# First RMS norm of a streaming encoder step: all squares on ScalarE, the depthwise weights' load moved behind the second half of the input, one weight tile's low parts on VectorE alone

## The chip, the cores and the metric

The kernel runs on one core of a Trainium2 chip. The metric is the device time of one execution in microseconds (us); the time before is the median of three runs. Engines are named as the profile names them: PE (TensorE matrix products; PEld is its weight load), DVE (VectorE), ACT (ScalarE), POOL (GpSimd) and SP (SyncE, which here only issues DMAs). Each engine works through its own queue in program order and waits on semaphores for the others.

## The reference

One inference step of a small encoder trunk: one layer with a convolution module and an FFN, one layer with chunked attention and an FFN, all in float32. What matters here is only its start:

```python
def rms_norm(x, g):
    xf = x.astype(jnp.float32)
    y = xf * lax.rsqrt(jnp.mean(xf * xf, axis=-1, keepdims=True) + EPS)
    return (y * g.astype(jnp.float32)).astype(x.dtype)

def conv_module(h, hist, g, w_pw1, b_pw1, w_dw, b_dw, ln_g, ln_b, w_pw2, b_pw2):
    a, gate = jnp.split(rms_norm(h, g) @ w_pw1 + b_pw1, 2, axis=-1)
    glu = a * jax.nn.sigmoid(gate)
    ...
```

The model width is 1024. There are 512 prompt frames and 8 x 16 sample frames, 640 columns in all. The depthwise convolution that follows uses the weights `w_dw` of width 31.

## The kernel before

Activations are kept with features on the 128 partitions: `h` is [128, 8, 640], so feature tile k (0 to 7) of a frame is one column. The 640 frames are worked on in two halves of 320 columns, g = 0 and g = 1.

**Products in three parts.** Every float32 operand is split into a high part (rounded to fp32r by ScalarE: `whi` for weights, L178; `xh` for activations, L190) and a low part (the difference, by VectorE: `wlo`, L183; `xl`, L192). A product is three PE matmuls, high x high, high x low and low x high (`mm3`, L202 to L204), each with 320 moving columns. `L243` are small matmuls that sum a norm's squares over the partitions, `L257` those that spread the resulting 1/rms back to all partitions, and `L149` (`warm`) are matmuls of the identity whose results nobody uses.

**First norm (`rms(0, ...)`, L298).** The input half g = 0 comes in four DMAs of two feature tiles each (`load_x`, L121, SP's queue). Each of the eight tiles is squared: by ScalarE (L211) where the letter in the string `SSQ` is `a`, by VectorE (L214) where it is `v`. VectorE adds the squares up in tile `acc` (L233). The squares' tiles `sq` rotate through two buffers, so that a square waits until the square two places before it has been added. Then: column sums on PE (L243), epsilon added on VectorE (L280, `rst`), power -0.5 on GpSimd (L287), spread on PE (L257), and for each k the scaled tile `n` on VectorE (L309), its `xh` on ScalarE and its `xl` on VectorE.

**Warm matmuls.** `WARM = 30, 9, 5, 0`: 30 identity matmuls stand in PE's queue ahead of the column sums, 9 between the sums and the spread, 5 behind the spread. Each is two records in the trace.

**Weights.** `w_pw1` comes in eight tiles of [128, 2048], `raw` (L164, SP's queue). The first two, `pws[0]` and `pws[1]`, are loaded and split in four pieces of 512 columns (`wsplit`, L152). The tuple `PL1` says how many quarters of a tile's low parts GpSimd takes in VectorE's place: for tile 1 it is 2, so of each piece VectorE makes 256 columns and GpSimd 256. The argument `ties` names earlier instructions behind which the split is to stand in its engines' queues; it sets an order, and adds no wait of its own.

**The first products.** `PLAN` (L75) starts with `a0 y x1 b0 b1`: `a0` is weight tile 0 with half 0 (48 matmuls), `y` loads input half 1 (`load_x(1)`, `in_xb`), `x1` is weight tile 1 with half 0 (48 matmuls), in whose middle the second half's norm is put (`mid`, L1056), and `b0`, `b1` are the same weight tiles with half 1. A scheduler with a time model of its own places the instructions in each engine's queue; PE takes the first half of `x1` in turn with `a0` and needs `n`, `xh` and `xl` of tile k as it goes. 72 matmuls of 320 columns stand between the spread and the second half's column sums (the second group of `L243`).

**The second half's norm (g = 1).** All eight squares are on ScalarE (`SSQ1`, L211), and GpSimd adds them up (L233, written as `w<-w,sq` in the trace since the sum is kept in a `w4` buffer). `behind(norm_end["xh"][2], ...)` puts these squares behind the third `xh` of the first half.

**The depthwise weights.** `dwv` [128, 504] is loaded by ScalarE's DMA queue (L781). In the trace it is first used by GpSimd at L890 (29.0 us).

Of the kernel before, what the change touches and what calls it, by code (L numbers as in the profile page):

```python
# [44 lines left out]
CUT, LCUT = 8, (7, 7)  # L45
GAPS, GAPS1 = (1, 12, 2), (5, 3, 12, 4)
POOLED = 14, 21, 26, W
PL1 = (0, 2, 0, 0, 0, 0, 0, 0)
PL2 = (0, 0)
M2 = ((0, 1, 2, 3), (2, 3, 0, 1))  # L50
SQ = 'aaaaaaaa'
# [1 line left out]
CVT = 4  # L53
HA = T + NB * SB - 320 - NB * SB
NXA, NXB = NB * SEG + HIST + HA, HIST + 320
SSQ = 'avavavaa'
SCUT = 8
CB, QB = 7, 1
NSTD = 3
# [10 lines left out]
SETS = "k1 v1 k2 k3 o0 k4 v2 k5 o1 k6 v3 k7 o2"  # L70
LAG = 1
SSQ1 = 'aaaaaaaa'
WARM = 30, 9, 5, 0
LNO = ((0, 1, 4, 5, 6, 3, 2, 7), (0, 1, 4, 2, 3, 5, 6, 7))
PLAN = ("a0 y x1 b0 b1 q0 dp1s0 c2 ds1p2 D3 C4 S3 q3 C5 E6 u S4 A4 F6 u k ds2 B4 E7 e S5 A5 F7 f k k k S6 A6 "  # L75
        "p S7 A7 n s0 m w1")
# [4 lines left out]
V_NKV, V_NATT, V_NFFN, V_NFIN, V_N = 56, 64, 72, 88, 96  # L81
# [4 lines left out]
def tile_trunk(ctx, tc, xT, vecs, hist, w_pw1, w_pw2, w_in0, w_out0, w_os0, w_in1, w_out1, w_os1,  # L86
               w_kq, w_v, w_o, rel, kc, vc, y_out, convp_out, convs_out, k_out, v_out):
    nc = tc.nc
# [27 lines left out]
    norm_end = {"xh": [], "n": [], "t": None}  # L116

    def load_x(g):
        g0, n = gr[g]
        for k in range(0, KT, 2):  # L120
            norm_end["x"] = nc.sync.dma_start(h[:, k:k + 2, g0:g0 + n], xT[g][:, k:k + 2, :]).ins  # L121
# [17 lines left out]
    @contextmanager  # L139
    def behind(*ins):  # L140
        with ExitStack() as st:
            for i in ins:
                st.enter_context(tc.issue_after(i))
            yield

    def warm(n):
        pt = mmt()
        for _ in range(n):
            end = nc.tensor.matmul(pt[:, 0:P], ident, ident, start=True, stop=True)  # L149
        return end.ins  # L150
# [43 lines left out]
    def new_xs(g):  # L194
        n = gr[g][1]
        return (xp.tile([P, KT, n], F32R, tag=f"xh{g}", name=nm("xh")),
                xp.tile([P, KT, n], F32R, tag=f"xl{g}", name=nm("xl")))
# [100 lines left out]
    def rms(g, gain, engs=SQ, cut=CUT, eng=nc.gpsimd, hold=None, hook=None):  # L298
# [3 lines left out]
        xh, xl = new_xs(g)  # L302
        if WARM[2 + g]:
            with behind(norm_spread[0]):
                warm(WARM[2 + g])
        for k in range(KT):
# [442 lines left out]
    dwv = cp.tile([P, V_NDW], F32, name="dwv", tag="dwv")  # L749

    def load_hist(c0, c1):
        nc.sync.dma_start(gs[:, c0:c1], hist[:, c0:c1])
# [17 lines left out]
    def first():  # L770
        with behind(mean_end[0]):
            warm(WARM[1])
        pws[0] = wsplit(w_pw1[0], 16, P, cuts=4, pool=PL1[0],
                        ties=[(norm_end["sq"], norm_end[e]) for e in ("acc", "acc", "rst", "rst")])

    with tc.issue_after(warm(WARM[0])), tc.high_priority(offset=2 * HP):
        xs = [rms(0, V_NCONV, SSQ, SCUT, nc.vector, hook=first), None]
    pws[1] = wsplit(w_pw1[1], 16, P, cuts=4, pool=PL1[1],
                    ties=(norm_end["sq"], norm_end["n"][3], norm_end["pow"]))
    load_hist(0, 2)  # L780
    nc.scalar.dma_start(dwv, vecs[:, V_N:])  # L781

    def w4t():
        return cp.tile([P, 1024], F32, tag="w4", name=nm("w4"), bufs=3)
# [256 lines left out]
    def step(op, arg):  # L1041
# [5 lines left out]
        elif op == "c":  # L1047
            w = pws.get(c) or wsplit(w_pw1[c], 16, P, pool=PL1[c], cuts=2)
            pws[c + 1] = wsplit(w_pw1[c + 1], 16, P)
# [2 lines left out]
            glu(c, 1, *w)  # L1052
        elif op == "y":
            load_x(1)
        elif op == "x":
            def mid(some):  # L1056
                def hook():
                    with tc.issue_after(mean_end[0]):
                        cover[:] = [some()]

                with behind(norm_end["xh"][2], norm_end["pow"]):
                    xs[1] = rms(1, V_NCONV, SSQ1, 8, hold=w4t, hook=hook)
            glu(1, 0, *pws[1], mid=mid)
        elif op in "CDEF":
            if op != "F":
# [73 lines left out]
    for tok in PLAN.split():  # L1139
        step(tok[0], tok[1:])  # L1140
# [459 lines left out]
    for p in range(NP):  # L1600
# [8 lines left out]
        for op in BO[p].split():  # L1609
# [11 lines left out]
            i = int(op[1]) if len(op) > 1 else None  # L1621
# [29 lines left out]
    with tc.high_priority(offset=HP):  # L1651
        sqs = xp.tile([P, KT, 384], F32, tag="xl1", name=nm("sqs")).rearrange("p a n -> p (a n)")
        acc, r = sqs[:, KT * NH:(KT + 1) * NH], sqs[:, (KT + 1) * NH:(KT + 1) * NH + 8]
        for k in range(KT):
            sq = square(h[:, k, 0:NH], NH, "a", sqs[:, k * NH:(k + 1) * NH])
# [103 lines left out]
    acc, bsb, bcs, sq, rs = {}, {}, {}, {}, {}  # L1759
# [117 lines left out]
```

## Time and profile before

| what | us |
|---|---|
| time before, median of three runs (1431.62 to 1432.91) | 1431.68 |
| the profiled execution's own time | 1431.78 |
| its span in the profile | 1430.0 |
| PE busy, share of the span | 1416.8, 99% |
| VectorE busy | 1113.5, 78% |
| ScalarE busy | 746.9, 52% |
| GpSimd busy | 278.4, 19% |

PE counts as busy in the warm matmuls too, and the ends of matmuls are modelled, so short waits hide in the 99%. The span is what the hardware profiler saw of the engines; 1.78 us of the profiled execution's time lie around it. A timeline row gives start, duration, engine, line, operation, output and inputs, shape and count; a row that merges several instructions gives their common stretch. In a bracket at a row's end stands how long the engine sat idle and what ended that.

### The profile page before, as it was taken

How to read it: one execution, taken by the hardware profiler on the slowest of the kernel's cores; microseconds unless marked ns; L12 is line 12 of the kernel's file. 1: busy time of each engine (PE TensorE's matmuls, PEld its weight loads, DVE VectorE, ACT ScalarE, POOL GpSimd, SP SyncE). 2: the span in 40 equal slices, each digit the busy share in tenths (PEclk: the TensorE clock that was granted, in tenths of full speed). 3: DMA queues.
4: the chain of work that ended last, by engine and by line, in shares of the span. 5: the costliest groups of instructions: out<-in, count | busy, mean ns of one | idle time of the engine just before them, and what ended most of it. 6: DMA issues, size and time to landing. Idle time of an engine off the chain costs nothing.

```text
span 1430.0 us, 28700 instructions
## 1 busy us (share of the span) xinstructions
PE 1416.8 (99%) x11076; PEld 1364.0 (95%) x11076; DVE 1113.5 (78%) x2490; ACT 746.9 (52%) x1633; POOL 278.4 (19%) x335
## 2 busy tenths in 40 slices
PE   9999999999999999999999999999999999999998
PEld 9998799999999999999998998888999999999998
DVE  7799867898888888765666757667898798798765
ACT  5666554554653554545654554544564564464453
POOL 5699121011111110112111111110011111111101
PEclk9999999999999999999999999999999999999999
DMA  7267424154644644524456555561244544554522
GB/s 248 91 176 187 123 84 143 32 122 122 169 107 121 148 115 117 139 89 174 165 185 205 187 179 173 181 218 51 60 108 118 147 125 110 145 131 109 135 72 74
DMA packets 93722, 192.62 MB, mean 135 GB/s; under 512 B 15121, under 2 KB 45585, under 8 KB 90129
## 3 DMA queue, kind: packets, MB, share of 16 engines
q1 hardware_dynamic: 79216, 160.59, 36.0%
q0 software_dynamic: 13504, 29.37, 10.5%
q8 instruction: 87, 1.43, 0.4%
q10 hardware_dynamic: 864, 0.83, 0.2%
q14 instruction: 51, 0.41, 0.1%
HBM read 179.14 MB, written 11.61 MB: 133 GB/s over the span
## 4 chain that ended last, share of the span: by engine, by line
PE 93%; DVE 4%; ACT 1%; issue 1%; DMA 1%; POOL 0%; DVEq 0%; ACTq 0%; POOLq 0%
PE mm L451 52%; PE mm L1311 11%; PE mm L202 6%; PE mm L204 6%; PE mm L203 6%; PE mm L923 3%; PE w L1311 2%; PE am L1484 1%; PE am L1556 1%; PE am L1500 1%; PE w L1455 1%; PE w L1518 1%; PE w L243 1%; PE mm L149 1%; PE w L257 1%
## 5 line engine op out<-in xcount | busy, mean ns | idle before, releaser
L451 PE MATMUL mm<-XH,whi 128*128 128x320 f32 x896 | 275.9, 310 | 1.0 <-ACT t L463 0.7
L451 PE MATMUL mm<-XH,wlo 128*128 128x320 f32 x896 | 276.2, 309 | 0.0
L451 PE MATMUL mm<-XL,whi 128*128 128x320 f32 x896 | 274.7, 309 | 0.0
L375 ACT ACTIVATE whi<-raw 128x512 fp32r<-128x512 f32 (+2 forms) x280 | 167.5, 613 | 148.4 <-PE mm L451 91.9
L376 DVE TENSOR_TENSOR wlo<-raw,whi 128x512 fp32r<-128x512 f32 (+2 forms) x280 | 183.8, 667 | 29.8 <-ACT whi L375 29.2
L451 PE MATMUL mm<-hid,whi 128*128 128x320 f32 x732 | 170.9, 310 | 0.0
L451 PEld LDWEIGHTS mm<-XH,whi 128*128 128x128 f32 x896 | 167.7, 188 | 2.8 <-ACT t L463 1.5
L451 PEld LDWEIGHTS mm<-XH,wlo 128*128 128x128 f32 x896 | 168.2, 188 | 0.0
L451 PEld LDWEIGHTS mm<-XL,whi 128*128 128x128 f32 x896 | 167.7, 188 | 0.0
L202 PE MATMUL mm<-xh,whi 128*128 128x320 f32 (+2 forms) x416 | 128.8, 312 | 0.5 <-DVE h L733 0.4
L203 PE MATMUL mm<-xh,wlo 128*128 128x320 f32 (+2 forms) x416 | 128.0, 309 | 0.0
L204 PE MATMUL mm<-xl,whi 128*128 128x320 f32 (+2 forms) x416 | 125.5, 310 | 1.0 <-DVE xl L192 1.0
L451 PEld LDWEIGHTS mm<-hid,whi 128*128 128x128 f32 x732 | 124.8, 188 | 1.5 <-DVE h L602 0.9
L451 PE MATMUL mm<-hid,wlo 128*128 128x320 f32 x366 | 113.0, 309 | 0.0
L451 PE MATMUL mm<-XH,shi 128*128 128x320 f32 x344 | 106.2, 310 | 1.2 <-DVE h L1588 0.7
L451 PE MATMUL mm<-XH,slo 128*128 128x320 f32 x344 | 106.0, 308 | 0.0
L602 DVE TENSOR_TENSOR h<-h,mm 128x320 f32<-128x320 f32 x168 | 79.1, 482 | 34.2 <-PE mm L451 34.2
L451 PE MATMUL mm<-XL,shi 128*128 128x320 f32 x344 | 105.6, 308 | 0.0
L375 ACT ACTIVATE shi<-raw 128x512 fp32r<-128x512 f32 (+1 forms) x114 | 66.4, 588 | 59.6 <-PE mm L451 31.6
L879 POOL TENSOR_TENSOR ca<-ca,cvt 128x512 f32<-128x512 f32 x60 | 89.5, 1492 | 17.3 <-ACT cvt L876 11.1
L428 POOL DMA_DIRECT2D s<-in_w_in x38 | 22.0, 578 | 309.1 <-ACT shi L375 67.3
L376 DVE TENSOR_TENSOR slo<-raw,shi 128x512 fp32r<-128x512 f32 (+1 forms) x114 | 72.0, 636 | 12.4 <-ACT shi L375 12.0
(337 smaller groups left out, 3663.1 us busy)
## 6 DMA issues: line engine op xcount, KB each, us to landing
raw<-in_w_in SPq DMA_DIRECT2D x152, 256.0 KB
s<-in_w_in POOLq DMA_DIRECT2D x76, 256.0 KB, 4.3
raw<-in_w_os SPq DMA_DIRECT2D x96, 192.0 KB
cache<-in_ck SPq DMA_DIRECT2D x32, 512.0 KB
cache<-in_cv SPq DMA_DIRECT2D x32, 512.0 KB
raw<-in_w_pw SPq DMA_DIRECT2D x11, 1024.0 KB
s<-in_w_os POOLq DMA_DIRECT2D x48, 192.0 KB, 3.6
raw<-in_w_kq SPq DMA_DIRECT2D x8, 1024.0 KB
```

What stands on the lines that cost most here:

```text
L149: end = nc.tensor.matmul(pt[:, 0:P], ident, ident, start=True, stop=True)
L202: nc.tensor.matmul(ps, wh, xh, start=(first and i == 0), stop=False)
L203: nc.tensor.matmul(ps, wl, xh, start=False, stop=False)
L204: end = nc.tensor.matmul(ps, wh, xl, start=False, stop=(stop and i == last))
L375: put_end[1] = nc.scalar.activation(out=hi, in_=src, func=AF.Copy).ins
L376: put_end[0] = nc.vector.tensor_tensor(out=lo, in0=src, in1=hi.bitcast(F32), op=sub).ins
L428: nc.gpsimd.dma_start(s1, src[:, 2 * n:3 * n])
L451: last = nc.tensor.matmul(pt, wt, v, start=(first and k == i == 0), stop=(k == n - 1 and i == 2), skip_group_check=True)
L602: hadd[i, u] = [nc.vector.tensor_tensor(out=hv, in0=hv, in1=pt, op=sub if row else add).ins]
L879: nc.gpsimd.tensor_tensor(out=acc, in0=acc, in1=pr, op=ALU.add)
L923: conv_end[0] = nc.tensor.matmul(pt[32 * q:32 * q + 32, 0:n], w4[0:r, 4 * tg + q, :], mv, start=(tg == 0), stop=(tg == 7)).ins
L1311: step_end[0] = nc.tensor.matmul(ps, w, x, start=i == j == 0, stop=i == len(wts) - 1 and j == 2).ins
```

## The change

Five places are edited.

- `SSQ` goes from `avavavaa` to `aaaaaaaa`: VectorE's three squares of the first norm go to ScalarE.
- `WARM[0]` goes from 30 to 21.
- `PL1[1]` goes from 2 to 0: GpSimd makes no low parts of weight tile 1 any more, VectorE makes all four pieces with 512 columns each.
- The ties of weight tile 1's split change: piece i (0 to 3) is placed behind `xh` of tile i + 1, where before all four pieces were placed behind the last square of the first norm.
- `dwv` is loaded on SP's queue behind the four DMAs of input half 1 (`y`), where it was on ScalarE's DMA queue at the program's start; and the second half's squares are placed behind the second `xh`, where they were behind the third.

```diff
-PL1 = (0, 2, 0, 0, 0, 0, 0, 0)
+PL1 = (0, 0, 0, 0, 0, 0, 0, 0)
-SSQ = 'avavavaa'
+SSQ = 'aaaaaaaa'
-WARM = 30, 9, 5, 0
+WARM = 21, 9, 5, 0
...
     pws[1] = wsplit(w_pw1[1], 16, P, cuts=4, pool=PL1[1],
-                    ties=(norm_end["sq"], norm_end["n"][3], norm_end["pow"]))
+                    ties=[(norm_end["xh"][i], norm_end["n"][3], norm_end["pow"])
+                          for i in range(1, 5)])
     load_hist(0, 2)
-    nc.scalar.dma_start(dwv, vecs[:, V_N:])
...
         elif op == "y":
             load_x(1)
+            nc.sync.dma_start(dwv, vecs[:, V_N:])
...
-                with behind(norm_end["xh"][2], norm_end["pow"]):
+                with behind(norm_end["xh"][1], norm_end["pow"]):
                     xs[1] = rms(1, V_NCONV, SSQ1, 8, hold=w4t, hook=hook)
```

What this makes of the queues shows best on VectorE, in the stretch where the first half's tiles are scaled and split (`n` scaled, `xl` low part, `wlo_239` or `wlo_230` the low part of weight tile 1). Before:

```order
L309 SCALAR_TENSOR_TENSOR n_23_213<-h,vec,w_2_137 128x320
L309 SCALAR_TENSOR_TENSOR n_24_217<-h,vec,w_2_137 128x320
L183 TENSOR_TENSOR wlo_239<-raw_237,whi_238 128x256 x4
L192 TENSOR_TENSOR xl_198<-n_23_213,xh_197 128x320
L192 TENSOR_TENSOR xl_198<-n_24_217,xh_197 128x320
L309 SCALAR_TENSOR_TENSOR n_25_221<-h,vec,w_2_137 128x320
```

VectorE, the same place of the changed program:

```order
L309 SCALAR_TENSOR_TENSOR n_23_204<-h,vec,w_2_128 128x320
L309 SCALAR_TENSOR_TENSOR n_24_208<-h,vec,w_2_128 128x320
L183 TENSOR_TENSOR wlo_230<-raw_228,whi_229 128x512
L192 TENSOR_TENSOR xl_189<-n_23_204,xh_188 128x320
L183 TENSOR_TENSOR wlo_230<-raw_228,whi_229 128x512
L192 TENSOR_TENSOR xl_189<-n_24_208,xh_188 128x320
L309 SCALAR_TENSOR_TENSOR n_25_212<-h,vec,w_2_128 128x320
L183 TENSOR_TENSOR wlo_230<-raw_228,whi_229 128x512
L309 SCALAR_TENSOR_TENSOR n_26_216<-h,vec,w_2_128 128x320
L192 TENSOR_TENSOR xl_189<-n_25_212,xh_188 128x320
L183 TENSOR_TENSOR wlo_230<-raw_228,whi_229 128x512
```

Four pieces of 256 columns in a row have become four pieces of 512 columns, spread among the low parts of tiles 2 to 4. On ScalarE, from the first weight tile's high parts (`whi_180`) on, before (`sq_347` and later are squares of the second half):

```order
L178 ACTIVATE whi_180<-raw_179 128x512 x4
L178 ACTIVATE whi_238<-raw_237 128x512 x4
L190 ACTIVATE xh_197<-n_21_205 128x320
L190 ACTIVATE xh_197<-n_22_209 128x320
L190 ACTIVATE xh_197<-n_23_213 128x320
L211 ACTIVATE sq_347<-h 128x320
L211 ACTIVATE sq_349<-h 128x320
```

ScalarE in the changed program (`whi_171` is weight tile 0, `whi_229` weight tile 1, `sq_334` the second half's first square):

```order
L178 ACTIVATE whi_171<-raw_170 128x512 x4
L190 ACTIVATE xh_188<-n_21_196 128x320
L190 ACTIVATE xh_188<-n_22_200 128x320
L178 ACTIVATE whi_229<-raw_228 128x512
L211 ACTIVATE sq_334<-h 128x320
L211 ACTIVATE sq_336<-h 128x320
L190 ACTIVATE xh_188<-n_23_204 128x320
L178 ACTIVATE whi_229<-raw_228 128x512
L190 ACTIVATE xh_188<-n_24_208 128x320
L178 ACTIVATE whi_229<-raw_228 128x512
```

The high parts of weight tile 1 have moved from ahead of the first `xh` to places between the `xh`, and the second half's first two squares stand ahead of the third `xh`. On GpSimd the four `L183` rows are gone and nothing else moves. On SP `dwv` stands behind the fourth `in_xb` load. On PE the same 72 products stand between spread and sums, with a few low-part products in other places. From there to the start of the first FFN every engine's order is the same; there, over some 500 of PE's 9219 rows, some rows change places with their neighbours, because the scheduler's time model had moved, and behind them the order is the same again.

## The prediction

> **What bounds the kernel now.** I read the span and the chain that ended last first, then who PE waited for (in all, how often, the longest).
>
> ```profile
> span 1430.0 us, 28700 instructions
> PE 93%; DVE 4%; ACT 1%; issue 1%; DMA 1%; POOL 0%; DVEq 0%; ACTq 0%; POOLq 0%
> PE mm L204 <- DVE xl L192: 1.0, 2, 0.5
> PE mm L451 <- DVE h L1588: 0.7, 1, 0.7
> ```
>
> The chain is PE's. Once its real products run, PE hardly stops: behind low parts `xl` twice, 0.5 each, and nowhere for more than 0.7. So the whole edit is worth what it does to one clock reading: the time at which PE has the first 72 products behind it and reaches the second half's column sums. What comes after keeps its length. The next view is the timeline of PE and its weight loads.
>
> ```profile
> 1.63 8.76 PEld L149 LDWEIGHTS mm<-ident 128*128 128x128 f32 x60 [1.63 <-POOL ident masks.py:199]
> 10.31 0.75 PEld L243 LDWEIGHTS w<-onec,acc 128*128 128x128 f32 x6
> 10.98 2.09 PEld L149 LDWEIGHTS mm<-ident 128*128 128x128 f32 x18
> 12.99 0.75 PEld L257 LDWEIGHTS w<-ident,rst 128*128 128x128 f32 x6
> 15.07 0.19 PEld L202 LDWEIGHTS mm<-xh,whi 128*128 128x128 f32 x1 [0.21 <-ACT xh L190]
> 27.13 0.72 PE L243 MATMUL w<-onec,w 128*128 128x1 f32 x6
> 38.46 0.31 PE L202 MATMUL mm<-xh,whi 128*128 128x320 f32 x1
> 43.89 0.31 PE L202 MATMUL mm<-xh,whi 128*128 128x320 f32 x1
> ```
>
> Real work starts at 15.07 and the second sums at **27.13**. The 60 warm records end where the first sums begin (10.31), and the 18 next ones where the spread begins (12.99): in both places PE's own queue, not only the data, sets the time. A product costs 0.147 (37 of them from 38.46 to 43.89), so 72 cost 10.6; 12.06 passed, and 1.5 were waits.
>
> **Part 1, the first norm sooner.** Behind the sums stand VectorE's additions; here is its timeline with ScalarE's squares and the load that is moved.
>
> ```profile
> 4.28 0.47 ACT L211 ACTIVATE sq<-h 128x320 f32<-128x320 f32 x1 [1.30 <-DMA h<-in_xa]
> 4.88 0.49 DVE L233 TENSOR_TENSOR acc<-sq,sq 128x320 f32<-128x320 f32 x1
> 5.98 0.49 DVE L214 TENSOR_TENSOR sq<-h 128x320 f32<-128x320 f32 x1 [0.61 <-DMA h<-in_xa]
> 6.48 0.49 DVE L233 TENSOR_TENSOR acc<-acc,sq 128x320 f32<-128x320 f32 x1
> 9.06 0.49 DVE L233 TENSOR_TENSOR acc<-acc,sq 128x320 f32<-128x320 f32 x1
> 9.65 0.49 DVE L233 TENSOR_TENSOR acc<-acc,sq 128x320 f32<-128x320 f32 x1
> 11.27 0.15 DVE L280 TENSOR_SCALAR rst<-w 128x3 f32<-128x3 f32 x1
> 11.50 1.25 POOL L287 TENSOR_TENSOR rst<-rst,mhalf 128x3 f32<-128x3 f32 x1 [8.93 <-DVE rst L280]
> 13.97 0.55 DVE L309 SCALAR_TENSOR_TENSOR n<-h,vec,w 128x320 f32<-128x320 f32 x1 [1.35 <-PE w L257]
> dwv<-in_vecs ACTq DMA_DIRECT2D x1, 252.0 KB
> 3.00:4.00 1.00, 1.00 (x7) 1.00 (x6) 0.00 (x0) 0.00 (x0) 0.00 (x0) 1.00 1.05 397
> ```
>
> The input's first pair of tiles is used at 4.28, the second at 5.98. From 3 us on the DMA engines are full at 397 GB/s, so `dwv` takes 258 KB / 397 = 0.65 us from the input. Without it the second pair comes between 5.33 (all of `dwv` was ahead) and 5.98 (none), the first between 3.63 and 4.28; I take 5.35 and 4.0, since both loads are issued in the same two microseconds.
>
> Now all squares are on ScalarE. Two of them and their sum take 4.0 + 0.41 + 0.47 + 0.05 + 0.49 = 5.4; the third square may then have its buffer and starts at 5.45, and the second addition at 5.95 (6.48 before). Five more follow. Additions that wait for ScalarE and for VectorE's own last result go 0.59 apart (9.06 to 9.65), and ScalarE with 0.47 a square keeps up. The last ends at 5.95 + 5 x 0.59 + 0.49 = **9.4 to 9.5**, before 10.14; the bounds are 9.05 and 9.9. Taking three squares (0.49 each) from VectorE thus brings less than their sum, for the slower pace takes part of it back.
>
> The 18 records fewer at 0.111 take 2.0 off the warm stretch: it ends near 8.35 and no longer sets anything, PE idles about 1.1 us. From the last addition to epsilon it is 11.27 - 10.14 = 1.13 (two low parts of weight tile 0 stand between), then 0.23 and 1.25 for the power: 9.45 + 2.61 = 12.06. On PE it is 0.67 for the sums and 2.01 for the nine warm ones: 9.5 + 2.68 = 12.18, a little later, as before. So spread, first `n` and first product come **0.8 sooner** (bounds 0.3 and 1.1): 12.18, 13.17, 14.27. The high parts of weight tile 1 that ScalarE no longer makes ahead of the first `xh` give nothing, since that `xh` waited for `n`.
>
> **Part 2, the products behind it.** VectorE must feed them, and it gets more to do. Its rows, ScalarE's and GpSimd's:
>
> ```profile
> 15.01 0.47 ACT L190 ACTIVATE xh<-n 128x320 fp32r<-128x320 f32 x1
> 17.14 0.82 ACT L211 ACTIVATE sq<-h 128x320 f32<-128x320 f32 x2
> 9.36 2.17 ACT L178 ACTIVATE whi<-raw 128x512 fp32r<-128x512 f32 x4
> 11.34 1.28 DVE L183 TENSOR_TENSOR wlo<-raw,whi 128x512 fp32r<-128x512 f32 x2
> 15.05 0.81 DVE L192 TENSOR_TENSOR xl<-n,xh 128x320 fp32r<-128x320 f32 x1
> 17.10 0.41 DVE L183 TENSOR_TENSOR wlo<-raw,whi 128x256 fp32r<-128x256 f32 x1
> 18.03 0.89 POOL L233 TENSOR_TENSOR w<-sq,sq 128x320 f32<-128x320 f32 x1 [2.52 <-ACT sq L211]
> 18.11 1.10 DVE L183 TENSOR_TENSOR wlo<-raw,whi 128x256 fp32r<-128x256 f32 x1
> 19.13 0.48 DVE L192 TENSOR_TENSOR xl<-n,xh 128x320 fp32r<-128x320 f32 x1
> 19.53 1.20 DVE L192 TENSOR_TENSOR xl<-n,xh 128x320 fp32r<-128x320 f32 x1
> 20.65 0.54 DVE L309 SCALAR_TENSOR_TENSOR n<-h,vec,w 128x320 f32<-128x320 f32 x1
> 21.11 0.54 DVE L309 SCALAR_TENSOR_TENSOR n<-h,vec,w 128x320 f32<-128x320 f32 x1
> 24.77 1.16 DVE L192 TENSOR_TENSOR xl<-n,xh 128x320 fp32r<-128x320 f32 x1
> 25.66 1.00 POOL L233 TENSOR_TENSOR w<-w,sq 128x320 f32<-128x320 f32 x1
> 29.00 1.91 POOL L890 TENSOR_TENSOR w<-i,dwv 128x1024 f32<-128x1024 f32 x1
> ```
>
> A low part takes 0.41 or 0.48 alone, and 1.1 to 1.2 when it starts just after one of GpSimd's sums (18.11 behind 18.03): it is held 0.70 until the sum is done; four were, the first at 18.11, the last at 24.77. `n`, which reads PSUM, is not held. From start to start VectorE pays 0.46 for an `n` (20.65 to 21.11), 0.40 for an `xl` (19.13 to 19.53), 0.34 for 256 columns of `wlo` (three from 17.10 to 18.11) and, two taking 1.28, 0.60 for 512. Before: 8 x 0.46 + 8 x 0.40 + 4 x 0.34 = 8.2 of the 11.96 from 13.97 to the last `xl`'s end, 24.77 + 1.16 = 25.93. The other 3.7 are four holds of 0.70, one of 0.33 behind GpSimd's low part (15.05), and 0.6 for `xh` and the like. Now the four `wlo` cost 2.4 in place of 1.36, in all **9.3**. GpSimd's low parts and the hold of 0.33 go; but the longer pieces stand where GpSimd's seven sums now run, from about 16 us on (the second `xh` still ends 1.5 behind the first `n`, at 14.7; then a high part of 2.17 / 4 = 0.54 and two squares, 0.82). I keep 3.7 (about half a hold more); the bounds are 2.8, four holds alone, and 4.9, all seven sums with one hold each. The last `xl` ends at 13.17 + 9.3 + 3.7 = 26.2 (25.3 to 27.4), **a quarter microsecond later than before although VectorE starts 0.8 sooner**.
>
> PE has three products behind the last `xl`: 0.06 to start (15.01, where one `xh` ends and the next begins, to the product's load at 15.07) + 3 x 0.147 = 0.5, so the second sums cannot start before 26.7 (25.8 to 27.9). Before, this floor was 26.4, and 27.13 came out, because PE had been stopped earlier (one of the two waits of 0.5, among others). With stops of that kind the new time lies between 26.7 and 27.3; I take 27.0, **0.1 sooner than 27.13**. Which end it is hangs on a race: whether VectorE's first 512-column piece or GpSimd's first sum starts first, both near 16.05.
>
> Of the rest: GpSimd's sums must be done by then; the last one ended at 26.66, 0.5 ahead of PE, and with the first one 2 us sooner (18.03 to 16.05) they end ahead of the last `xl`, hidden. `dwv` now follows the second half's input, which the row at 25.66 shows to have been there before; 0.65 more is still ahead of 29.0, where GpSimd first reads it. PE's other wait of 0.5 comes in the second half's products, whose queues keep their order, and stays. The new order of rows at the first FFN moves products among neighbours whose inputs PE did not wait for; I cost it at nothing, and bound it by the longest wait that PE has there or anywhere behind the start, 0.7, to the bad side and 0.2 to the good one.
>
> The Trainium skill, "SBUF — State Buffer", section "Who interferes with whom", says that a VectorE instruction with two SBUF inputs and a GpSimd instruction that reads SBUF exclude each other, the later one blocking until the first is done. By that rule all twelve two-input parts are exposed, not only those that met a sum before; with seven sums it gives the upper bound above. The held rows agree with it (1.10 in place of 0.41).
>
> **The rivals.**
>
> 1. *The start's gain stays* (chance 0.2). The race goes VectorE's way throughout, with four holds or fewer, and PE reaches the sums at 25.9 to 26.5: 1430.4 to 1431.0. For it speaks that PE's floor leaves room; against it that VectorE has 1.0 more to do.
> 2. *VectorE becomes the bound, slower* (0.15). Six or seven sums hold a low part; each hold beyond the fifth puts 0.70 on the last `xl`. From the sixth on it decides: PE at 27.4 to 27.9, 1432.0 to 1432.5.
> 3. *PE's clock drops in the new idle microsecond* (0.04). At the start the same warm records come at half the pace:
>
> ```profile
> 5.00:6.00 1.00, 1.00 (x7) 1.00 (x7) 0.39 (x2) 0.02 (x1) 0.00 (x0) 1.00 1.05 371
> 6.00:7.00 1.00, 1.00 (x12) 1.00 (x11) 0.97 (x2) 0.45 (x1) 0.00 (x0) 1.00 0.99 339
> ```
>
> 7 records in a microsecond and, from 6 us, 12. If the 1.1 us without work brought that back, the 24 records to the spread would cost 24 x 0.1 = 2.4 more, the start would come 1.6 later than before, and up to 2 us more would go in the products: 1433 to 1435. The trace has two stops of 0.5 and products 0.147 apart behind the second; nothing as long as 1.1 is in it. The Trainium skill, "TensorE: Matmul & The Clock Gate", section "What's actually happening", puts the fall at an idle window of about 3.4 us; by that rule 1.1 us costs nothing.
> 4. *The first norm does not move* (0.06): `dwv` took nothing from the input, and additions at 0.59 end at 9.9. The start gains 0.3, VectorE's 9.3 + 3.7 stay, and the second sums come at 27.3 to 27.8: 1431.9 to 1432.3.
>
> **How the numbers follow.** The profiled execution took 1431.78 (the span and 1.78 around it), 0.1 above the median of the three runs, 1431.68. PE's reading of 27.0 takes 0.1 from either: I forecast **1431.6** on the median, with a chance of 0.55 and 1431.0 to 1432.0 of its own. The range takes rival 1 with the lower FFN bound and the lowest run, and rivals 2 and 4 with the upper FFN bound and the spread of the runs: 1430.0 to 1433.2. A measurement of this kernel tells about 0.2%, 2.9 us, from no change. The gain on hand is at most 1.1 at the start and 1.5 of waits, so *faster* needs all of both and more: 0.02. *Slower* needs rival 3 at its worst or an unseen stop: 0.04. *Same*: 0.94.
>
> **What would show it.** In the changed kernel's profile: the last first-half addition ending at 9.4 to 9.5, the first product near 14.3, low parts of 1.1 us and more beside GpSimd's sums, the last first-half `xl` ending near 26.2, and second sums near 27.0. Additions 0.5 apart, or a second pair at 4.9, would make part 1 too small; sums at 26 would show VectorE's waits overrated; warm records 0.21 apart behind 9 us would be rival 3; a new PE stop between 200 and 400 us, the FFN's order.

## The result, and the profile after

The changed kernel takes 1435.81 us (median of 11 runs, 1433.31 to 1436.63); the kernel before, beside it on the same chip, 1431.59 (1430.95 to 1432.91). The ratio is **1.0025, 95% interval 1.0015 to 1.0034**: slower by some 3.6 us, clear of the noise, though with a quarter of a per cent still inside what the forecast called *same*. I had forecast 1431.6 with a range up to 1433.2. The profiled execution is the shortest of the 11: 1433.31, with a span of 1431.4. It therefore shows only part of the loss, and a second one was needed (below).

The page of the changed kernel, span and chain, and then whom PE waited for:

```profile
span 1431.4 us, 28664 instructions
PE 91%; DVE 4%; DMA 2%; ACT 1%; issue 1%; POOL 0%; SPq 0%; DVEq 0%; ACTq 0%
```

```profile
PE mm L204 <- DVE xl L192: 1.2, 2, 0.8
PE w L243 <- DVE acc L233: 0.7, 1, 0.7
```

36 instructions fewer are the nine matmuls taken out (each two weight loads and two matmuls). The chain's DMA share went from 1% to 2%, which asks for a transfer that had not been waited for. The waits for low parts are about what they were (1.2, before 1.0), and the one ahead of the sums is the idle time of the start. First the start, on PE and VectorE:

```profile
1.62 7.18 PE L149 MATMUL mm<-ident 128*128 128x128 f32 x42 [1.62 <-POOL gall L761]
9.48 0.83 PE L243 MATMUL w<-onec,acc 128*128 128x1 f32 x6 [0.67 <-DVE acc L233]
12.37 0.93 PE L257 MATMUL w<-ident,rst 128*128 128x128 f32 x6
14.45 0.41 PE L202 MATMUL mm<-xh,whi 128*128 128x320 f32 x1
26.98 0.72 PE L243 MATMUL w<-onec,w 128*128 128x1 f32 x6
7.14 2.28 DVE L233 TENSOR_TENSOR acc<-acc,sq 128x320 f32<-128x320 f32 x4 [0.20 <-ACT sq L211]
21.31 1.36 DVE L183 TENSOR_TENSOR wlo<-raw,whi 128x512 fp32r<-128x512 f32 x1
24.24 1.67 DVE L192 TENSOR_TENSOR xl<-n,xh 128x320 fp32r<-128x320 f32 x2
```

The additions end at 7.14 + 2.28 = 9.42, the first product starts at 14.45, the last low part ends at 25.91, the second sums start at 26.98. The start came out close to the forecast, and up to 470 us PE stays 0.1 to 0.3 ahead of the kernel before. The time goes at two places of the first FFN. PE there, and the chain into the second place:

```profile
477.56 0.31 PE L451 MATMUL mm<-XL,whi 128*128 128x320 f32 x1
478.34 0.42 PE L451 MATMUL mm<-XH,whi 128*128 128x320 f32 x1 [0.47 <-ACT whi L375]
478.95 0.42 PE L451 MATMUL mm<-XH,shi 128*128 128x320 f32 x1 [0.19 <-DVE h L602]
589.92 0.31 PE L451 MATMUL mm<-XL,whi 128*128 128x320 f32 x1
590.69 0.41 PE L451 MATMUL mm<-XH,shi 128*128 128x320 f32 x1 [0.46 <-ACT shi L375]
591.29 0.41 PE L451 MATMUL mm<-XH,whi 128*128 128x320 f32 x1 [0.19 <-DVE h L602]
```

```profile
584.82 4.59 DMA raw<-in_w_in
589.49 0.64 ACT whi L375
```

Products that should follow 0.15 apart start 0.78 and 0.61 apart (0.77 and 0.60 at the second place): 0.94 and 1.0 lost against the kernel before. PE waits for a high part that ScalarE makes (L375) of a weight block loaded by SP (L424), 4.59 from issue to landing. ScalarE's rows show how much later that load is; the first pair is the kernel before, the second the changed one:

```profile
476.53 0.63 ACT L375 ACTIVATE shi<-raw 128x512 fp32r<-128x512 f32 x1 [2.69 <-DMA raw<-in_w_in]
587.87 0.63 ACT L375 ACTIVATE whi<-raw 128x512 fp32r<-128x512 f32 x1 [2.60 <-DMA raw<-in_w_in]
```

```profile
477.14 0.63 ACT L375 ACTIVATE shi<-raw 128x512 fp32r<-128x512 f32 x1 [3.62 <-DMA raw<-in_w_in]
589.49 0.63 ACT L375 ACTIVATE whi<-raw 128x512 fp32r<-128x512 f32 x1 [3.61 <-DMA raw<-in_w_in]
```

ScalarE idles 3.6 instead of 2.6. At the first place the trace has fifteen of the load's sixteen parts landed by 475.71 and the last at 477.07. At the second place the fifteenth lands 3.52 behind the issue and the last 4.59. What is new beside the load is a packet of the kind *instruction*, on queue q8, taken here to be PE's own program (the runs below test that). The DMA view between 586.8 and 587.8 of the changed kernel (packets, then queue and kind: packets, MB, share of 16 engines):

```profile
DMA packets 166, 0.32 MB, mean 324 GB/s; under 512 B 16, under 2 KB 16, under 8 KB 165
q8 instruction: 1, 0.02, 5.5%
```

One packet of 16 KB, 5.5% of 16 engines for 1.0 us, or 0.88 us of one engine. It starts at 586.85, 2.0 behind the load's issue. Before, the packet started at 583.17, 1.0 ahead of the issue (584.20).

### The profile page after: what moved, and what is told of

Read it like the earlier page. It is cut to its first block, busy times and chain, and to the rows that moved or that the text cites. A ratio compares the mean times of both kernels' runs of the same rounds, so it can differ in the third digit from the quotient of the medians.

```text
span 1431.4 us, 28664 instructions
## 1 busy us (share of the span) xinstructions
PE 1416.0 (99%) x11058; PEld 1362.3 (95%) x11058; DVE 1113.0 (78%) x2487; ACT 747.2 (52%) x1636; POOL 275.4 (19%) x331
## 4 chain that ended last, share of the span: by engine, by line
PE 91%; DVE 4%; DMA 2%; ACT 1%; issue 1%; POOL 0%; SPq 0%; DVEq 0%; ACTq 0%
PE mm L451 51%; PE mm L1312 11%; PE mm L202 6%; PE mm L204 6%; PE mm L203 6%; PE mm L923 3%; PE w L1312 2%; PE am L1485 1%; PE am L1557 1%; PE am L1501 1%; PE w L1456 1%; PE w L1519 1%; DMA raw<-in_w_in 1%; PE w L243 1%; DVE wlo L376 1%
## 5 line engine op out<-in xcount | busy, mean ns | idle before, releaser
L375 ACT ACTIVATE whi<-raw 128x512 fp32r<-128x512 f32 (+2 forms) x280 | 167.8, 613 | 150.3 <-PE mm L451 92.8
L375 ACT ACTIVATE shi<-raw 128x512 fp32r<-128x512 f32 (+1 forms) x114 | 66.3, 588 | 62.8 <-PE mm L451 33.4
```

Source lines behind the costliest of these rows:

```text
L375: put_end[1] = nc.scalar.activation(out=hi, in_=src, func=AF.Copy).ins
```

## The experiments

The theories, by the letters of the expectations. **A**: PE's program is fetched in such packets; with fewer instructions ahead of a point, the packet fetched there comes later against the work, and now meets a weight load that PE needs soon. **B**: the idle time at the start lowers PE's clock. **C**: the rest of the change costs the time. **D**, from the third set on: PE's clock falls to half for one stretch of 3.41 us when PE does little for about half of such a stretch, at the start and elsewhere. Every kernel was timed in 11 runs except two (8 and 5). The edits are against the change, unless another base is named.

**The change once more, and three kernels on its warm matmuls.** The first has the change unedited.

> The changed kernel once more. Theory A (PE's instruction fetch): two groups of PE stops, near 478 and 590 us, 0.6 to 0.8 each, behind a weight load whose last part lands 1.3 late on one DMA engine while a 16 KB instruction packet passes; they alone make 1433.3. Theory B (PE's clock falls in the new idle microsecond at 8.5 to 9.5): most executions are 1434.6 to 1436.6 and show PE products 0.29 apart in place of 0.147 for some 3.4 us, near the start. Rival C (the start itself): second sums later than 27.2 in the slow executions, without either.

Measured: 1434.87 (1433.25 to 1436.52), ratio 1.0020 [1.0011, 1.0029]. The profile is of its longest execution, 1436.52, and shows what the first one lacked. Stretches of 1 us: PE, PEld, DVE, ACT, POOL, then the granted clock, the DMA share and GB/s:

```profile
590.00:591.00 1.00, 0.68 (x5) 0.42 (x3) 0.00 (x0) 0.02 (x1) 0.00 (x0) 1.00 0.73 133
593.00:594.00 1.00, 1.00 (x4) 1.00 (x5) 1.00 (x3) 0.63 (x2) 0.00 (x0) 0.50 0.00 0
594.00:595.00 1.00, 1.00 (x5) 1.00 (x5) 1.00 (x2) 0.52 (x1) 0.00 (x0) 0.50 0.12 8
596.00:597.00 1.00, 1.00 (x8) 1.00 (x7) 1.00 (x3) 0.33 (x2) 0.31 (x1) 0.88 0.17 61
```

The packet here took 2.05 us, the high part started 5.7 behind the load's issue, and PE stopped for 1.81 and 0.60. Then the clock was 0.5 from 592.82 to 596.24, and four or five products went into a microsecond instead of seven. This place alone cost 3.5; another 0.4 went at 478, and 0.5 at 316.

```diff
-WARM = 21, 9, 5, 0
+WARM = 30, 9, 5, 0      # warm30
+WARM = 21, 18, 5, 0     # count
```

> The changed kernel with 30 warm matmuls in place of 21; all else as in the change, and the order at the first FFN is then that of before. PE has as many instructions ahead of every later place as before, and no idle microsecond ahead of the first sums. A: no stops at 478 and 590. B: no slow executions, all within 1.5. First sums near 10.3, first product near 15.1, second sums 27.3 to 27.8, so 1431.7 to 1432.3. Rival C: as slow as the change, 1435 to 1436.

Measured: 1432.39 (1431.92 to 1437.14), ratio 1.0011 [1.0002, 1.0020]; no stop at 478 or 590, though the first sums come at 10.96. The second sums come at 28.60, later than the 27.3 to 27.8 expected. Two of the 11 runs take 1436.20 and 1437.14, at a mean clock of 0.998; neither was profiled, so what lengthens them is open.

> The changed kernel with 21 warm matmuls ahead of the first sums and 18 in place of 9 behind them: the idle microsecond stays, PE has the 30 instructions of before in all, and the other engines have the order of the 30-warm kernel. The nine cost 2.0 at the start: second sums 28.4 to 29.2, 1432.9 to 1433.6 by that alone. A: no stops at 478 and 590. B: the slow executions stay, median 2 to 3 above that, 1435 to 1436.5.

Measured: 1434.15 (1433.27 to 1435.95), 1.0015 [1.0006, 1.0024]. The idle time ahead of the sums is there (1.30), and the first product (16.84) comes 2.4 later, for the nine stand in the way; no stop at 478 or 590. Two things differ from the expectation: the second sums (29.84) are later, and PE waits 0.94 for a DMA (`xa`) at 155, where the kernel before doesn't. The time lies above A's expectation and below B's.

```diff
-    def warm(n):
+    def warm(n, last=0):
...
-        for _ in range(n):
-            end = nc.tensor.matmul(pt[:, 0:P], ident, ident, start=True, stop=True)
+        for i in range(n):
+            c, mv = (KT * HIST, gp[:, :, 0:HIST]) if i >= n - last else (P, ident)
+            end = nc.tensor.matmul(pt[:, 0:c], ident, mv, start=True, stop=True)
...
-    with tc.issue_after(warm(WARM[0])), tc.high_priority(offset=2 * HP):
+    with tc.issue_after(warm(WARM[0], 6)), tc.high_priority(offset=2 * HP):   # wide: the last six of the 21 move 240 columns
```

> The changed kernel with 21 warm matmuls, the last six with 240 columns of zeros in place of 128 of the identity, so that the warm stretch ends near 9.5 and the idle microsecond is filled while the number of PE instructions stays that of the change. A: the stops at 478 and 590 stay, 1433.0 to 1433.8. B: no executions above 1434; median 1433.3. If B is wrong, median 1435.8 as in the change.

Measured: 1435.41 (1434.02 to 1436.47), 1.0023 [1.0014, 1.0032]. Little idle time at the start (0.21 ahead of the sums), yet stops of 0.79 and 0.61 at 478 and of 0.43 and 0.61 at 591. So the stops go with the number of PE's instructions and not with the idle time: against B as the cause of the stops. The time is above A's 1433.0 to 1433.8. Part of that is no doing of the packets: the profiled execution loses another 1.1 at 296 and 307, in an order of the FFN's rows that the change itself doesn't have.

**Parts alone.** The kernel before with 21 warm matmuls and nothing else of the change:

```diff
-WARM = 30, 9, 5, 0
+WARM = 21, 9, 5, 0
```

> The kernel before with 21 warm matmuls in place of 30 and nothing else of the change. Theory A (PE's program is 9 matmuls shorter, so its instruction packets come some 4 us earlier against the weights and delay a weight piece at about 478 and 590 us): the stops of 0.6 to 0.8 at 478 and 590 appear although the first norm is the old one; 1433 to 1436, near the change's 1434.9. Theory B (the idle time in the start's warm stretch lowers PE's clock): the idle time is longer than the change's (sums at 10.3, warm matmuls done by 7 to 8), no stops at 478 and 590, time lost at the start alone, warm or first products at half pace. Theory C (the rest of the change: squares, split, load order): within 0.5 of 1431.7, no stops.

Measured: 1433.72 (1431.38 to 1436.90), 1.0016 [1.0007, 1.0025]; stops of 1.99 and 0.60 at 590, none at 478. In the profiled execution (1433.72) this one number, of nine matmuls whose result nobody uses, brings the larger of the two stops. Three of the 11 runs take no more than 1432.16, so the loss does not come in full every time. The expectation had the direction wrong: the packets come later, not earlier (+1.9 against the issue instead of -1.0).

```diff
-WARM = 21, 9, 5, 0
+WARM = 30, 1, 5, 0      # late
```

> The change with 30 warm matmuls ahead of the sums but 1 in place of 9 between sums and spread: PE's program is 8 matmuls shorter than before's behind the spread, where the change's is 9 shorter. Nothing idles ahead of the sums for long. Theory A: the stops at 478 and 590 come as in the change, 1433 to 1436. Theory B (idle time of 0.7 us ahead of the sums): no stops, 1431 to 1432.5.

Measured: 1435.37 (1432.87 to 1437.83, 8 runs), 1.0026 [1.0016, 1.0036]; stops of 0.55 and 0.60 at 590, none at 478. Another 1.1 goes at 296 and 307: this kernel has the same order of the FFN's rows as wide. The profiled execution is the shortest of the eight (1432.87), so what the others lose beyond that isn't shown.

Next, only the squares on ScalarE and the later `dwv`; the rest as before, with 30 and with 26 warm matmuls:

```diff
-PL1 = (0, 0, 0, 0, 0, 0, 0, 0)
+PL1 = (0, 2, 0, 0, 0, 0, 0, 0)
-WARM = 21, 9, 5, 0
+WARM = 30, 9, 5, 0      # split30; 26 in split26
...
-                    ties=[(norm_end["xh"][i], norm_end["n"][3], norm_end["pow"])
-                          for i in range(1, 5)])
+                    ties=(norm_end["sq"], norm_end["n"][3], norm_end["pow"]))
...
-                with behind(norm_end["xh"][1], norm_end["pow"]):
+                with behind(norm_end["xh"][2], norm_end["pow"]):
```

> Only the squares on ScalarE and the later load of the depthwise weights; 30 warm matmuls, GpSimd's quarters of weight tile 1, the ties and the second half's squares as before, so PE's and GpSimd's queues are the same as before. If the change's longer stretch from first product to second sums (12.5 to 13.0 against 12.06) comes of the VectorE low parts, the stretch is 12.0 to 12.3 here; if it comes of the clock's rise or of the depthwise load, it stays 12.5 or more. Theory A: no stops at 478 and 590; time 1431.0 to 1432.2.

Measured: 1431.24 (1430.30 to 1432.37), 0.9995 [0.9986, 1.0004]; no stops. First product 15.88, second sums 27.66: 11.78 between them, below even the 12.0 to 12.3 expected. VectorE's groups between first `n` and last `xl`, before, then the changed kernel (busy time, mean ns of one):

```profile
L192 DVE TENSOR_TENSOR xl<-n,xh 128x320 fp32r<-128x320 f32 x8 | 6.0, 786 | 0.2
L183 DVE TENSOR_TENSOR wlo<-raw,whi 128x256 fp32r<-128x256 f32 x4 | 2.1, 583 | 0.0
```

```profile
L192 DVE TENSOR_TENSOR xl<-n,xh 128x320 fp32r<-128x320 f32 x8 | 5.6, 703 | 0.1
L183 DVE TENSOR_TENSOR wlo<-raw,whi 128x512 fp32r<-128x512 f32 x4 | 3.6, 910 | 0.0
```

The longer `wlo` add 1.5, the `xl` give 0.4 back. With the new low parts the stretch from first product to second sums is 12.5 in two profiles (the change's first one and late) and 13.0 in the other eight (among them the change's second one, warm30, wide and count); with the old ones it is 11.8 to 12.1. So this part of the change costs 0.5 to 0.9, about what the earlier start of 0.6 brings, and more often a little above it.

> As the run with only squares and load moved, with 26 warm matmuls, so that PE is free for the sums at about 9.5. Theory A: PE's packets come 4 matmuls' worth earlier, half of the change's shift; whether they meet the weight pieces at 478 and 590 isn't known beforehand: stops of under 0.8 there or none; with none, first product near 14.4, second sums at 26.4 to 26.7 and 1430.9 to 1431.4, faster than both; with stops, 1432.5 to 1435.

Measured: 1432.87 (1431.48 to 1433.58), 1.0006 [0.9997, 1.0015]. Second sums at 26.50, but stops of 0.50 and 0.60 at 590 and 1.1 lost at 295 and 306, with the order of late and wide.

**Number and place of the instructions apart.** The runs so far change the order of the FFN's rows along with the number. Here nine matmuls of one column (same instructions, hardly any columns) are put back, either as the last nine of 30 warm ones, which restores the FFN's order of before but for one row, or ahead of the first FFN's seventh weight block:

```diff
-    def warm(n):
+    def warm(n, narrow=0):
...
-        for _ in range(n):
-            end = nc.tensor.matmul(pt[:, 0:P], ident, ident, start=True, stop=True)
+        for i in range(n):
+            c = 1 if i >= n - narrow else P
+            end = nc.tensor.matmul(pt[:, 0:c], ident, ident[:, 0:c], start=True, stop=True)
...
-    with tc.issue_after(warm(WARM[0])), tc.high_priority(offset=2 * HP):
+    with tc.issue_after(warm(WARM[0], 9)), tc.high_priority(offset=2 * HP):   # narrow9, snarrow9, with WARM[0] = 30
...
+            for _ in range(9 * (len(filled) == 6)):      # fill, with WARM[0] = 21
+                nc.tensor.matmul(pa[:, 0:1], ident, ident[:, 0:1], start=True, stop=True)
```

> The change with 30 warm matmuls of which the last nine have one column in place of 128: as many instructions on PE as before and the first FFN's order of before (the order differs from before's only around the start and by one row there), but PE free for the sums at about 9.5 or 10, so the start is that of the change. Theory A (the place of PE's instruction packets against the weights): packets at about 470 and 583.3, no stops at 478 and 590, 1431.0 to 1432.2. Theory C (what the change does to the start, squares, splits, load order, costs the time): 1434 to 1436 as the change.

Measured: 1433.19 (1431.60 to 1434.87), 1.0005 [0.9996, 1.0013]. No stop at 478, 0.53 at 590 (0.3 lost). But in the profiled execution (1433.37) the clock is 0.5 from 11.87 to 15.28, and first product and second sums come at 16.14 and 29.12. So the expected 1431.0 to 1432.2 was missed, for a reason that A doesn't hold.

> The same 30 warm matmuls, nine of them with one column, with only the squares on ScalarE and the later load of the depthwise weights (weight tile 1's low parts, ties and second half's squares as before). First sums at 9.4 to 10.0, stretch from first product to second sums 11.8 to 12.1 as in the run with squares and load alone, second sums 26.0 to 26.6, no stops at 478 and 590: 1430.5 to 1431.2, below before and the change.

Measured: 1431.60 (1430.52 to 1433.07), 0.9995 [0.9986, 1.0004]; stretch 11.77, no stops at 478 and 590. The first sums (10.30), the second sums (26.81) and the time all came a little later than expected. The profiled execution, its longest, has a stop of 2.0 at 152, behind the same DMA (`xa`) as in count, that the kernel before lacks.

> The change with its 21 warm matmuls and its order up to the first FFN's seventh weight block kept, and nine one-column matmuls of the identity put there, ahead of 470 us. Theory A: from there on PE's packets are back where they were before, near 583.3 in place of 586.1 by the kernel's own time, no stop at 590; the nine cost about 1; 1433 to 1434 in profile terms, without the runs at 1435 and above. If the first FFN's order or the start were the cause, the stop at 590 stays and the time is that of the change plus 1, 1436.

Measured: 1433.55 (1432.93 to 1436.90), 1.0014 [1.0005, 1.0022]. The change's order up to that block, its 21 warm matmuls, and no stop at 478 or 590: ScalarE idles 2.49 for the load, much as before (2.60). The nine one-column matmuls took 2.0, from 391.83 to 393.75, and not the 1 expected.

```profile
591.55 0.63 ACT L376 ACTIVATE whi<-raw 128x512 fp32r<-128x512 f32 x1 [2.49 <-DMA raw<-in_w_in]
```

The runs above 1435 did not go: there are three, and the profiled one, 1435.87, shows the start:

```profile
8.00:9.00 1.00, 0.00 (x0) 0.00 (x0) 0.79 (x3) 0.88 (x3) 0.00 (x0) 1.00 1.03 393
10.00:11.00 1.00, 1.00 (x11) 1.00 (x11) 1.00 (x4) 1.00 (x2) 0.18 (x1) 1.00 1.03 395
12.00:13.00 1.00, 1.00 (x6) 1.00 (x6) 0.00 (x0) 0.00 (x0) 0.06 (x1) 0.50 1.06 396
13.00:14.00 1.00, 1.00 (x7) 1.00 (x6) 0.00 (x0) 0.00 (x0) 0.00 (x0) 0.50 1.06 379
```

The clock had risen early here, at 4.47 (6.31 in the change's profile), so the 42 warm records end at 7.92 and PE idles 1.60 until 9.52. From 11.29 to 14.71 the clock is 0.5, and the second sums come at 28.84. The four runs with a mean clock of 0.998 take 1434.34 to 1436.90, the other seven 1432.93 to 1433.73.

```diff
-WARM = 21, 9, 5, 0
+WARM = 21, 1, 4, 0      # minus18
```

> The change with 21, 1 and 4 warm matmuls, 18 fewer than before where the change has nine fewer. Theory A with a window: the packet that meets the weights at 590 moves on by about as much again, to 588 to 591, behind the load (issued at 584.8, landed by 588), and the stop at 590 goes or shrinks below 0.3 although the program is still shorter; at 478 the packet comes at 476 to 478, likewise past. If fewer instructions are bad by themselves, both stops stay or grow.

Measured: 1437.86 (1437.15 to 1441.17, 5 runs), 1.0042 [1.0029, 1.0056]. Its start loses time (clock 0.5 from 14.14 to 17.55, behind 1.44 of waiting for the spread's input), as do other places. But the two stops are gone, as the window form of A said, though the program is the shortest of all:

```profile
591.88 0.63 ACT L375 ACTIVATE whi<-raw 128x512 fp32r<-128x512 f32 x1 [2.43 <-DMA raw<-in_w_in]
```

A stop of the same kind stands at a third place instead, where no other profile has one:

```profile
369.50 0.63 ACT L375 ACTIVATE whi<-raw 128x512 fp32r<-128x512 f32 x1 [3.81 <-DMA raw<-in_w_in]
370.70 0.41 PE L451 MATMUL mm<-XH,whi 128*128 128x320 f32 x1 [0.66 <-ACT whi L375]
371.31 0.41 PE L451 MATMUL mm<-XH,whi 128*128 128x320 f32 x1 [0.19 <-DVE h L602]
```

A packet starts there at 366.92, 2.3 behind the issue of the load (364.63); fifteen of the load's parts land within 3.53 of the issue and the last at 4.79. The rows of the first FFN stand in this kernel in the order of before but for a few, so the stop needs neither the change's order nor those two places.

All profiles together, from the records of each trace. "Packet" is its start less the issue of the load, "part" the start of the high part less that issue, in us, at the first and the second place; "took" is the duration of the second place's packet:

| run | packet, part at 478 | packet, part at 590 | took | stops |
|---|---|---|---|---|
| before | -2.8, 3.7 | -1.0, 3.7 | 1.1 | none |
| split30 | -2.0, 3.7 | -1.0, 3.6 | 1.0 | none |
| fill | -2.3, 3.4 | -1.1, 3.6 | 0.9 | none |
| split26 | -0.7, 3.7 | +1.2, 4.4 | 1.0 | 590 |
| late | -0.7, 3.6 | +1.8, 4.5 | 0.9 | 590 |
| wide | +1.5, 4.7 | +1.7, 4.3 | 0.9 | 478, 590 |
| change | +1.4, 4.7 | +2.0, 4.7 | 0.9 | 478, 590 |
| change, second | +0.8, 4.1 | +2.1, 5.7 | 2.0 | 478, 590 |
| before21 | +0.9, 3.8 | +1.9, 5.9 | 2.4 | 590 |
| minus18 | +3.2, 3.5 | +4.0, 3.5 | 1.5 | none |

A packet that starts 0.8 to 2.1 behind the issue makes the part late, by 0.2 to 1.1 at the first place and at the second by about as long as the packet takes (0.7 to 1.1, and 2.1 to 2.3 for the two long ones); ahead of the issue, or 3 and more behind it, it does next to nothing. The other seven profiles (warm30, count and those with narrow matmuls but fill) have the packet 1.0 to 1.1 ahead of the issue at 590 and the part at 3.4 to 3.7, but for narrow9: 4.0, and the 0.53. That one is not explained by its packet: narrow4's and snarrow4's reach as far past the issue, with the part at 3.5 and 3.4, and in narrow9 two of the load's parts land late (3.83 and 3.89) and not one.

All the traces' loads of the FFN's weights (`in_w_in`, SP's queue) say the same. Where no q8 packet starts between 2.5 ahead of the issue and 6 behind it (1581 loads), the last part lands 0.13 behind the fifteenth at the median, and over 0.6 behind it in 7% of them. Where one packet starts in that stretch, 0.8 to 2.3 behind the issue (114 loads), the median is 0.76, and 61% are over 0.6. Most of these delays cost nothing: the kernel before has six of the 114 loads, three of them over 0.6, and PE nowhere waits more than 0.2 beside them.

The size of the shift fits where 36 and 72 instructions are missing, and is too small for 16: at two instructions for each product of 0.147, 16, 36 and 72 instructions fewer are 1.2, 2.6 and 5.3 us of work (an estimate), and the packet at 590 moved by 2.2, 2.7 to 3.1 and 5.0.

**What was open then:** whether the fall of the clock at the start belongs to the cause. Nine one-column matmuls in the kernel before (bnarrow9); the change, and squares and load alone, with only the last four of 30 narrow (narrow4, snarrow4):

```diff
-    with tc.issue_after(warm(WARM[0])), tc.high_priority(offset=2 * HP):
+    with tc.issue_after(warm(WARM[0], 9)), tc.high_priority(offset=2 * HP):   # bnarrow9, on the kernel before; 4 in the others
```

> The kernel before with its 30 warm matmuls, the last nine with one column in place of 128: same instructions, same packets, same start of the sums (10.2 to 10.6), but PE has little to move in the last 2 us ahead of them. Theory D (PE's clock falls to half for 3.41 us when PE moves little for about half of such a stretch): in a share of the executions, some 3 to 8 of 11, the clock falls between 10 and 16 us and these take 1.5 to 2.5 longer, 1433.3 to 1434.5, the others stay at 1431 to 1432.5; no stops at 478 and 590. Without D: all within 1 of the kernel before.

Measured: 1432.52 (1430.82 to 1435.10), 1.0007 [0.9998, 1.0015]. Five of 11 runs lie between 1433.29 and 1435.10, within the expected share; but the profiled one is the shortest, 1430.82, without a fall, so that D makes those five is not shown. Their mean clocks are mixed: 0.997 and 0.998 in three of them, 0.999 and 1.000 in two. A fall of 3.41 us takes 0.0012 off the mean, so at least the run with 1.000 (1433.60) had none and was long for another reason.

> The change with 30 warm matmuls, the last four with one column: packets as before (583.1 by the kernel's own time), less than 1 us of little work ahead of the sums, first sums at 10.0 to 10.8. Theory A with D (stops at 478 and 590 from the packets, falls of the clock from the little work): neither happens, 1431.8 to 1432.6, and fewer runs above 1433.3 than with nine such matmuls (5 of 11). If more of the change than these two costs time: 1433 or more.

Measured: 1432.41 (1431.85 to 1434.56), 1.0005 [0.9997, 1.0014]; ten of 11 runs at or below 1432.97, no stops, no fall of the clock. The second sums come at 27.72, 0.6 later than before (first sums 9.99, stretch 12.99).

> Only the squares on ScalarE and the later load, 30 warm matmuls of which the last four have one column. Stretch from first product to second sums 11.7 to 12.0, first sums 10.0 to 10.8, no stops at 478 and 590, no fall of the clock at the start: 1430.8 to 1431.6, below the kernel before and the change by 0.3 to 1 and by 3.

Measured: 1431.51 (1429.82 to 1433.15), 0.9997 [0.9988, 1.0006]; stretch 11.83, no stops. The time is only 0.2 below the kernel before, not 0.3 to 1.

With the moved packets and the idle time both taken out, the change is thus 0.7 above the kernel before (1431.68 beside it; the interval takes in 1), and its second sums alone are 0.6 late; with both in, it was 3.1 and 4.2 above. split30, snarrow9 and snarrow4 lie 3 to 4 below the change. Against the kernel before all three intervals take in 1, so none is shown to beat it.

## Why the prediction was wrong

**Part 1 held.** Last addition at 9.42 (9.4 to 9.5 forecast), first product at 14.45 (14.27), so 0.6 sooner and not 0.8. That the additions ended to the tenth where forecast is in part luck: the second one started 0.1 earlier than in the sum (5.84), and a wait of 0.20 for the third pair of tiles, which the sum did not have, took it back. Rival 4, a first norm that does not move, fell.

**Part 2 held in mechanism, with a size off.** The last `xl` ended at 25.91 (26.2 forecast), the second sums came at 26.98 (27.0) and 27.31 in the other execution. Work and waits on VectorE took 12.56 (13.35 to 25.91), not 13.0. The stretch behind the first product, 12.73 by the forecast, was 12.5 here but 13.0 in eight of the ten profiles with the new low parts, and the race that the prediction names decides most of it. In this execution VectorE's first piece starts 0.3 ahead of GpSimd's first sum and takes 0.68; late is alike. In seven of the others the sum starts some 0.04 ahead and the piece takes 1.38 or 1.39. The change first, then wide:

```profile
16.22 0.68 DVE L183 TENSOR_TENSOR wlo<-raw,whi 128x512 fp32r<-128x512 f32 x1
16.55 1.08 POOL L233 TENSOR_TENSOR w<-sq,sq 128x320 f32<-128x320 f32 x1 [4.23 <-ACT sq L211]
```

```profile
16.47 1.39 DVE L184 TENSOR_TENSOR wlo<-raw,whi 128x512 fp32r<-128x512 f32 x1
16.43 0.88 POOL L234 TENSOR_TENSOR w<-sq,sq 128x320 f32<-128x320 f32 x1 [3.94 <-ACT sq L212]
```

The change's second profile has the piece 0.05 ahead and 13.0 all the same. So the 27.0 was met by an execution that won the race, and is some 0.3 early for most. Of the two rivals next to it, the gain that stays did not come; a slower VectorE came near, with second sums at 27.31 where rival 2 has 27.4 to 27.9.

**The step that failed is the first one: "What comes after keeps its length."** The warm matmuls were priced by their own time alone (2.0 off the warm stretch). Taken out, they also moved PE's instruction packets by 3 us against everything behind them, and at 478 and 590 us a packet met a weight load with no slack. That cost 1.9 in the execution of 1433.31. In that of 1436.52 the stops at 590 were 1.8 and 0.6, and the clock fell behind them: 3.5 at that place. before21 shows that the nine matmuls are enough for the stop at 590, fill and minus18 that neither the FFN's order nor a shorter program as such makes it, and minus18's stop at 371 that a packet behind a load is enough. Why a packet takes 0.9 us in one execution and 2 in another stays open; of the 3.2 between the two profiled executions, 2.6 come from the place at 590.

The median itself, 4.2 above, is not a profiled execution. The mean clocks point to more falls: the seven runs of 11 at 0.998 take 1435.46 to 1436.63, the four at 0.999 take 1433.31 to 1434.64. At half the clock 3.41 us give half their work, so one fall is worth up to 1.7 (an estimate). Where in those seven runs the clock fell isn't shown. The second timing splits less cleanly (three at 0.998, one of 1436.22 at 0.999).

**The FFN's new order**, costed at nothing with a bound of 0.7, cost nothing in one execution and 0.5 (at 316 us) in the other. The profile was to show it by a stop between 200 and 400 us; the stops that counted came later and had another cause. The bound was not safe all the same: the order that wide, late and split26 share cost 1.1.

**Rival 3** (the clock drops) had a chance of 0.04 because the idle time was taken as 1.1 in every execution and held too short. Both were too simple: it was 0.67, 1.06 and 1.60 in three executions with these 21 warm matmuls, since it depends on when the clock rises, and 1.60 was enough. Neither of the change's own two profiles has the fall at the start, so how often it happens there isn't shown.

## What to carry to other kernels

Taking out instructions that cost nothing is not free: it moves the program's own packets against the loads behind them, so a load that a busy engine needs at once had better be issued with more than a packet's duration to spare (no run here tried that). Where a result differs from the sum, follow the offset of the two traces along the whole span before reading any stage (here it was flat up to 470 us and stepped at two points), and profile a second execution if the runs spread as widely as the loss.

## What the hardware showed

- Instruction packets of 16 KB on queue q8 run beside the weight loads. A packet that starts 0.8 to 2.3 us behind a load's issue goes with one of the load's sixteen parts landing late, at 590 us by 0.7 to 1.1 for packets of 0.9 to 1.0 and by 2.1 to 2.3 for packets of 2.0 and 2.4. That packet and part share one of the sixteen DMA engines is inferred from this; the traces don't name the engine. The Trainium skill, "DMA: Bandwidth & Descriptors", section "Queues, rings and completion order", says that a DMA engine takes its queues in turn, packet by packet; the delay of about one packet's duration agrees with that.
- PE's clock rose at 4.47 to 7.52 us in the 17 profiles, and with it the end of the same warm matmuls moved. Every fall inside a kernel came a whole number of stretches of 3.413 us behind the rise: 2 in fill, narrow9 and minus18, 172 in the change's second profile (587.09), and it lasted one stretch.
- In the stretch before the fall PE had idled 1.60 us (fill), 1.69 (1.50 and 0.19, the change's second profile) and 1.44 (minus18), less than half of 3.413 each; in narrow9 it had not idled, but had nine one-column matmuls there. 1.37 (snarrow9, from 152.53) brought no fall, and neither did 1.65 in the second-last whole stretch of the kernel before (from 1422.35), so idle time alone does not settle it. In before21 a longer stop (1.99 and 0.60 from start to start, 1.87 of it idle) brought no fall: a border between stretches, at 590.15 (the rise at 6.47 and 171 times 3.4133), leaves 1.28 of it in one stretch. The Trainium skill, "TensorE: Matmul & The Clock Gate", section "What's actually happening", has the window of 3413 ns that runs freely, which agrees, and a fall after at least one idle window; here less than half a window was enough, so the measurement decides.
